# Start, gate rows and last norm of a two-layer encoder trunk: first weight chunk in two DMAs, written order, earlier row loads, TensorE in the last LayerNorm

## The chip, the cores and the metric

The kernel runs on one core of a Trainium2 chip. The metric is the device time of the whole program in microseconds (us), as the median of three runs. A profiled execution has a span (first to last instruction) and a time of its own beside it.

## What is computed

The reference takes 256 frames of width 2048 through two layers. Layer 0 mixes with a gated MLP (gelu, a LayerNorm over 6144 gate channels, a 128x128 masked product over positions, a product with the other half, an output projection); layer 1 with a low-rank attention. After each mixer comes a gated MLP with a causal convolution of width 3. Each sub-layer ends in a LayerNorm. All in float32:

```python
z = gelu(x @ w_in); u, v = split(z, 2)
v = layer_norm(v, ln_g, ln_b)
s = einsum('gij,bnjgd->bnigd', w_s * mask, v) + b_s
m = (u * s) @ w_out                       # layer 0; layer 1: latent attention
x = layer_norm(ALPHA * x + m, ln_mix_g[i], ln_mix_b[i])
f = (silu(conv(x @ w_up)[g]) * conv(x @ w_up)[a]) @ w_down
x = layer_norm(ALPHA * x + f, ln_ffn_g[i], ln_ffn_b[i])   # the last one writes the output
```

## The kernel before, in words

**Products.** Every float32 weight is split on the core into a rounded part (`wh`, a cast on ACT, L131) and a remainder (`wl`, a subtraction on DVE, L134); activations are split in the same way (`xhl` holds both parts side by side). A product is then three TensorE matmuls: hi by hi, lo by hi, hi by lo (`prod_b`, called by `Banks.to`). Some chunks are "seven" chunks, which trade one of eight products for sums of weights made on DVE (`ts`, L141) and split too (`th`, `tl`). 128 rows by 512 columns is one PSUM bank, and eight banks exist.

**Weights.** All weights pass through one list of chunks of 1 MB (`Feed`). SyncE (SP) loads chunk i into one of three `raw` buffers (`_load`, L88 on), ACT and DVE split it (`_split`), TensorE uses it. A load may start when the buffer is free, that is when chunk i-3 has been split, and not before the matmul that was written last ahead of it (`behind`). DVE, ACT and SP each work strictly in the order of their queue; a scheduler makes the order, and some instructions are pinned in the written one.

**Start.** A bf16 tile of zeros is set by GpSimd (POOL), and nine matmuls on it run while nothing has been loaded (L286 on). Then, for the first quarter of x (j = 0), SP is given in this order: x of k = 0; pieces 1 and 2 of chunk 0 (512 columns each); x of k = 1; pieces 3 and 4; x of k = 2 and of k = 3; then chunk 1 in two halves. The interleaving is done by two callbacks, `feed.between` (L324), which `_load` and `_split` call after their second piece. Chunk 0 holds the weights of k = 0 (columns 0 to 1023) and k = 1 (1024 to 2047), chunk 1 those of k = 2 and 3. The 24 matmuls of a chunk are `acc.eight`, in an order that the scheduler chose. POOL also loads the first quarter of the position weights (`wT`, from `in_w_sT_dram`) at that time, through its own software queue.

**The gate v and its rows.** Six groups g of 1024 columns of v are made first (chunks 0 to 47), then six groups of u (chunks 48 to 95). `stats(gi)` (L707) sums the squares of v of one group on ACT; its output tiles are not read, and lie in the pool `t2` of five buffers, which also holds the temporaries of a group's end (`rest`, L442). After the sums of the last group come mean and reciprocal deviation (`mv`, `vrs`). `row_v` (L783) has POOL load one row of 512 of the gate LayerNorm's scale or shift, spread over all partitions, into a `t2` tile `vr`; `norm_v` (L796 and L797) normalises v with them on DVE, in two passes: (v - mean) by scale row, then by `vrs` and plus shift row. For g = 0, these stand before the products of u; for the later groups among them. `spatial(0)` is the position product of group 0 (matmuls on `wT`), behind the third chunk of u (chunk 50). At the end of group 0 of u, `rest` reads four banks on DVE (L448 to L451), and the next group's matmuls write into these banks.

**The end.** The last down projection is finished one row block b (128 frames) and one quarter f (512 columns) at a time. `piece` (L661, L664) adds a quarter to the residual and takes its moments; after the last quarter, `start` aggregates them (L669), ACT takes the square root and DVE the reciprocal; `scale` (L678, L679) is, per quarter, (r - mean) by the scale row `lng` and then by the reciprocal deviation and plus the shift row `lnb`, and SP stores the quarter.

## Time and profile before

| | |
|---|---|
| median of 3 runs | 2469.26 us (2468.65, 2469.26, 2470.97) |
| profiled execution: its own time | 2471.25 us |
| profiled execution: span | 2469.5 us |
| mean granted TensorE clock | 0.998 |
| TensorE (PE) busy | 2453.7 us, 99% of the span, 12481 instructions |
| VectorE (DVE) busy | 2054.2 us, 83% |
| ScalarE (ACT) busy | 1459.5 us, 59% |
| moved from and to HBM | 544.75 MB read, 65.06 MB written |

In a timeline row the first number is the start in us from the span's start, the second the time from the first start to the last end of the instructions in the row, then engine, line, operation, output and inputs, and the count; in brackets stands how long the engine had been idle before it, and what released it. A wait row names the waiting engine and line, what it waited for, the total, the number of waits and the longest. PE is the matmul part of TensorE, PEld its weight loads.

### The profile page before, as it was taken

The numbers are of one execution on the slowest core, as the hardware profiler recorded it, in microseconds if no ns is written. First come the engines' busy times: TensorE is split into PE (matmuls) and PEld (weight loads), VectorE is DVE, ScalarE is ACT, GpSimd is POOL, SyncE is SP. The second block draws the span as 40 slices with busy tenths as digits, with TensorE's granted clock in tenths as the row PEclk, the third lists the DMA queues.
The fourth block names the chain that finished last, engine by engine and source line by source line (L and its number), as shares of the span: only waits on it lengthen the run. The fifth ranks groups of instructions, "written<-read, shape, count | busy, mean of one in ns | idle before, by whom it ended". The sixth has DMA issues, their size and how long they took to land. (4 is left out here: it accounts for less than half of the span.)

```text
span 2469.5 us, 32459 instructions
## 1 busy us (share of the span) xinstructions
PE 2453.7 (99%) x12481; PEld 2091.0 (85%) x12481; DVE 2054.2 (83%) x2734; ACT 1459.5 (59%) x1969; POOL 104.2 (4%) x202
## 2 busy tenths in 40 slices
PE   9999999999999999999999999999999999999998
PEld 7888788888888888888888888988888888888886
DVE  7999899889898788788777897867598787878798
ACT  6666565566565666556655566665565665655453
POOL 0000000000000000000000000000000000000000
PEclk9999999999999999999999999999999999999999
DMA  7555766656665678777868885544478787877885
GB/s 276 204 205 208 231 204 194 217 181 213 206 219 190 230 291 322 297 279 288 330 215 320 303 300 184 193 158 161 172 270 310 273 312 294 300 264 274 300 324 201
DMA packets 117004, 611.94 MB, mean 248 GB/s; under 512 B 10712, under 2 KB 11488, under 8 KB 75760
## 3 DMA queue, kind: packets, MB, share of 16 engines
q1 hardware_dynamic: 90704, 462.47, 52.7%
q0 software_dynamic: 26144, 147.39, 15.9%
q8 instruction: 98, 1.61, 0.3%
q14 instruction: 58, 0.48, 0.1%
HBM read 544.75 MB, written 65.06 MB: 247 GB/s over the span
## 5 line engine op out<-in xcount | busy, mean ns | idle before, releaser
L134 DVE TENSOR_TENSOR wl<-raw,wh 128x1024 fp32r<-128x1024 f32 (+4 forms) x645 | 957.3, 1499 | 176.8 <-ACT wh L131 131.8
L131 ACT CAST wh<-raw 128x1024 fp32r<-128x1024 f32 (+4 forms) x645 | 809.3, 1278 | 362.6 <-PE up L236 85.7
L236 PE MATMUL up<-xhl,wh 128*128 128x512 f32 x2624 | 611.4, 390 | 0.0
L236 PEld LDWEIGHTS up<-xhl,wh 128*128 128x128 f32 x2624 | 487.5, 188 | 97.7
L236 PEld LDWEIGHTS up<-xhl,wl 128*128 128x128 f32 x2624 | 325.8, 192 | 6.4
L236 PE MATMUL up<-xhl,wl 128*128 128x256 f32 x2624 | 328.1, 283 | 0.0
L131 ACT CAST th<-ts 128x1536 fp32r<-128x1536 f32 (+1 forms) x138 | 142.8, 1052 | 113.8 <-DVE ts L141 89.4
L236 PE MATMUL ub<-wh,xhl 128*128 128x512 f32 x576 | 179.5, 393 | 1.9 <-DVE u0w L449 1.9
L134 DVE TENSOR_TENSOR tl<-ts,th 128x1536 fp32r<-128x1536 f32 (+1 forms) x138 | 162.9, 1217 | 10.5 <-ACT th L131 3.6
L236 PEld LDWEIGHTS ub<-wh,xhl 128*128 128x128 f32 x576 | 108.1, 188 | 26.4 <-DVE u0w L449 2.4
L236 PE MATMUL ub<-wl,xhl 128*128 128x512 f32 x288 | 112.2, 389 | 0.0
L141 DVE TENSOR_TENSOR ts<-ts,raw 128x512 f32<-128x512 f32 x138 | 94.5, 684 | 1.4
L141 DVE TENSOR_TENSOR ts<-raw 128x1024 f32<-128x1024 f32 x69 | 84.0, 1218 | 7.7 <-PE ub L236 3.8
L236 PE MATMUL mo<-wh,oT 128*128 128x512 f32 x256 | 82.5, 401 | 0.0
L236 PE MATMUL v_q<-wh,xhl 128*128 128x512 f32 x224 | 70.1, 394 | 1.7 <-ACT wh L131 1.7
L236 PEld LDWEIGHTS ub<-wl,xhl 128*128 128x128 f32 x288 | 54.1, 188 | 11.4
L236 PE MATMUL v_p<-wh,xhl 128*128 128x512 f32 x192 | 60.2, 392 | 0.1
L236 PEld LDWEIGHTS v_q<-wh,xhl 128*128 128x128 f32 x224 | 42.2, 190 | 11.3 <-ACT wh L131 2.7
L236 PEld LDWEIGHTS mo<-wh,oT 128*128 128x128 f32 x256 | 45.5, 189 | 7.1
L236 PE MATMUL mo<-wl,oT 128*128 128x512 f32 x128 | 50.1, 392 | 0.0
L693 ACT ACTIVATE lny<-lnt,lncol 128x128 f32<-128x128 f32 x96 | 36.5, 469 | 15.7 <-PE lnt L689 15.6
L396 DVE TENSOR_TENSOR h_0a<-up,lo_0a 128x256 f32<-128x256 f32 x41 | 17.2, 419 | 32.7 <-ACT lo_0a L394 32.7
(1826 smaller groups left out, 4328.4 us busy)
## 6 DMA issues: line engine op xcount, KB each, us to landing
raw<-in_ffn_up_dram SPq DMA_DIRECT2D x172, 1024.0 KB, 7.1
raw<-in_gm_in_dram SPq DMA_DIRECT2D x93, 1024.0 KB, 5.3
raw<-in_ffn_dn_dram SPq DMA_DIRECT2D x68, 1024.0 KB, 6.9
raw<-in_gm_wout_dram SPq DMA_DIRECT2D x48, 1024.0 KB, 5.2
praw<-in_ffn_dn_dram POOLq DMA_DIRECT2D x16, 1024.0 KB, 15.2
keptth<-pth POOLq DMA_DIRECT2D x16, 1024.0 KB, 8.1
kepttl<-ptl POOLq DMA_DIRECT2D x16, 1024.0 KB, 9.0
fth<-keptth POOLq DMA_DIRECT2D x16, 1024.0 KB, 10.0
```

The lines of the kernel that those rows point to most:

```text
L131: cast = self.nc.scalar.copy(hi, raw)
L134: self.nc.vector.tensor_tensor(lo, raw, hi.bitcast(F32), ALU.subtract)
L141: add = lambda o, a, b: self.nc.vector.tensor_tensor(o, a, b, ALU.add)
L236: recent[0] = nc.tensor.matmul(o, l, r, start=start, stop=stop, skip_group_check=True)
L396: nc.vector.tensor_tensor(h, acc[:, 0:S], lo, ALU.add)
L693: nc.scalar.activation(y[:, j], t[:, j * P : (j + 1) * P], AF.Identity, bias=lncol[:, o : o + 1], scale=lncol[:, g : g + 1])
```

## The change

There are three places.

**Start.** Chunk 0 is loaded in two DMAs of 1024 columns instead of four of 512 and still split in four pieces; x of k = 0 and 1 comes in one DMA ahead of it, x of k = 2 and 3 in one behind it; the callbacks are gone. There are ten matmuls on zeros instead of nine. The matmuls of chunks 0 and 1 (the "first two pairs") are pinned in a written order, `Banks.first`: for each half of the chunk and each 512 columns in it, hi by hi for both row blocks, lo by hi for both, hi by lo for both.

SP's queue at the start of the program, before (`xraw` is x as loaded, `raw` a weight chunk):

```order
L315 DMA xraw_90<-in_xT_dram 128x256
L102 DMA raw_92<-in_gm_in_dram 128x512 x2
L315 DMA xraw_90<-in_xT_dram 128x256
L102 DMA raw_92<-in_gm_in_dram 128x512 x2
L315 DMA xraw_90<-in_xT_dram 128x256 x2
L102 DMA raw_118<-in_gm_in_dram 128x1024 x2
L315 DMA xraw_121<-in_xT_dram 128x512 x2
```

and in the changed kernel:

```order
L310 DMA xraw_91<-in_xT_dram 128x512
L100 DMA raw_93<-in_gm_in_dram 128x1024 x2
L310 DMA xraw_91<-in_xT_dram 128x512
L100 DMA raw_111<-in_gm_in_dram 128x1024 x2
L310 DMA xraw_114<-in_xT_dram 128x512 x2
```

The bytes and their order are the same but for x of k = 1, which has moved ahead of chunk 0; ten DMAs up to the end of chunk 1 have become six.

**Gate rows.** `row_v` for group 0 is called ahead of `stats(5)`, and `stats(5)` writes its unread squares into four PSUM banks of the coming u products (`ub[4:]`) instead of into `t2` tiles. So the rows take the buffers that the temporaries of v's last group leave, not those that the squares leave.

DVE's queue behind the last group of v, before (`v_462` is group 0 of v, `v_774` group 1, `vmv` the means, `vrs` the reciprocal deviations, `vr` the rows, `raw_1950` chunk 51, `raw_2055` chunk 52):

```order
L359 RECIPROCAL vrs_2015<-vrs0q 128x1
L796 SCALAR_TENSOR_TENSOR v_462<-v_462,vmv_2005,vr_2027 128x512
L796 SCALAR_TENSOR_TENSOR v_462<-v_462,vmv_2006,vr_2027 128x512
L797 SCALAR_TENSOR_TENSOR v_462<-v_462,vrs_2015,vr_2029 128x512
L359 RECIPROCAL vrs_2025<-vrs1q 128x1
L796 SCALAR_TENSOR_TENSOR v_462<-v_462,vmv_2005,vr_2031 128x512
L797 SCALAR_TENSOR_TENSOR v_462<-v_462,vrs_2025,vr_2029 128x512
L797 SCALAR_TENSOR_TENSOR v_462<-v_462,vrs_2015,vr_2033 128x512
L796 SCALAR_TENSOR_TENSOR v_462<-v_462,vmv_2006,vr_2031 128x512
L134 TENSOR_TENSOR wl_2082<-raw_1950,wh_2081 128x2048
L797 SCALAR_TENSOR_TENSOR v_462<-v_462,vrs_2025,vr_2033 128x512
L141 TENSOR_TENSOR ts_2115<-raw_2055 128x1024
```

and in the changed kernel (`v_455` is group 0, `v_767` group 1, `raw_1943` chunk 51); two first passes over `v_455` stand just ahead of this piece:

```order
L831 SCALAR_TENSOR_TENSOR v_767<-v_767,vmv_2010,vr_2100 128x512
L821 TENSOR_SCALAR vmv_2011<-vmv_2011 128x2
L822 TENSOR_TENSOR vmv_2011<-vmv_2011,vc 128x1
L831 SCALAR_TENSOR_TENSOR v_455<-v_455,vmv_2011,vr_1998 128x512
L823 TENSOR_TENSOR vmv_2011<-vmv_2011 128x1
L831 SCALAR_TENSOR_TENSOR v_455<-v_455,vmv_2011,vr_2002 128x512
L824 TENSOR_TENSOR vmv_2011<-vmv_2011 128x1
L128 TENSOR_TENSOR wl_2071<-raw_1943,wh_2070 128x2048
L351 RECIPROCAL vrs_2020<-vrs0q 128x1
L831 SCALAR_TENSOR_TENSOR v_767<-v_767,vmv_2011,vr_2100 128x512
L351 RECIPROCAL vrs_2030<-vrs1q 128x1
L832 SCALAR_TENSOR_TENSOR v_455<-v_455,vrs_2020,vr_2000 128x512
```

The first passes have moved ahead of the reciprocals, the split of chunk 51 ahead of the second passes, and a pass over group 1 that needs the fifth row (`vr_2100`) ahead of all of these. ACT's cast of chunk 51 likewise stands ahead of the square roots now.

**Last norm.** For the last row block, `finish` replaces `scale`. With mean m, reciprocal deviation s, scale row g and shift row b, three of the four quarters are computed as r g s + (b - m s g): `weigh` multiplies r by g ahead of the last quarter's piece; TensorE puts b into three PSUM banks by a float32 product with the identity, and adds -m s g by a float32 product with a diagonal matrix `dg`; one pass on DVE per quarter then joins the two. The fourth quarter takes the two passes of before.

DVE's queue from the last two pieces on, before:

```order
L661 TENSOR_TENSOR res_1_20724<-res_1_20724,dn_e 128x512
L664 BN_STATS lnst_1_19367<-res_1_20724 128x6
L661 TENSOR_TENSOR res_1_20724<-res_1_20724,dn_q_20199 128x512
L664 BN_STATS lnst_1_19367<-res_1_20724 128x6
L669 BN_AGGR lnmv_1_21011<-lnst_1_19367 128x2
L678 SCALAR_TENSOR_TENSOR res_0_19894<-res_0_19894,lnmv_1_21011,lng_20772 128x512
L359 RECIPROCAL lnrs_1_21015<-lnrs_1q 128x1
L678 SCALAR_TENSOR_TENSOR res_0_19894<-res_0_19894,lnmv_1_21011,lng_20772 128x512
L679 SCALAR_TENSOR_TENSOR res_0_19894<-res_0_19894,lnrs_1_21015,lnb_20774 128x512 x2
L678 SCALAR_TENSOR_TENSOR res_1_20724<-res_1_20724,lnmv_1_21011,lng_20772 128x512 x2
L679 SCALAR_TENSOR_TENSOR res_1_20724<-res_1_20724,lnrs_1_21015,lnb_20774 128x512 x2
```

and in the changed kernel:

```order
L688 TENSOR_TENSOR res_1_20713<-res_1_20713,lng_20761 128x512
L664 TENSOR_TENSOR res_1_20713<-res_1_20713,dn_q_20188 128x512
L667 BN_STATS lnst_1_19356<-res_1_20713 128x6
L672 BN_AGGR lnmv_1_21009<-lnst_1_19356 128x2
L351 RECIPROCAL lnrs_1_21013<-lnrs_1q 128x1
L699 SCALAR_TENSOR_TENSOR off<-lnmv_1_21009,lnrs_1_21013 128x1
L701 TENSOR_SCALAR dg<-ident,off 128x128
L705 SCALAR_TENSOR_TENSOR res_1_20713<-res_1_20713,lnmv_1_21009,lng_20761 128x512
L706 SCALAR_TENSOR_TENSOR res_1_20713<-res_1_20713,lnrs_1_21013,lnb_20763 128x512
L710 SCALAR_TENSOR_TENSOR res_0_19883<-res_0_19883,lnrs_1_21013,fin_21003 128x512
L710 SCALAR_TENSOR_TENSOR res_0_19883<-res_0_19883,lnrs_1_21013,fin_21004 128x512
L710 SCALAR_TENSOR_TENSOR res_1_20713<-res_1_20713,lnrs_1_21013,fin_21005 128x512
```

Eight passes over 512 columns behind the aggregation have become five, with two small operations ahead of them; three multiplications have moved ahead of the last piece. TensorE has six float32 products more at its end.

The diff, cut to its core:

```diff
@@ Feed._load
-        step = 512 if self.loaded == 0 else cols
...
-            if self.loaded in (1, 2):
-                step = 1024
+            step = 1024 if self.loaded < 3 else cols
             for o in range(0, cols, step):
                 self.behind(self.nc.sync.dma_start(t[:, o : o + step], ap[:, o : o + step]))
-                if self.loaded == 0 and o == step:
-                    self.between[0]()
@@ Feed._split
-            if i == 0 and o == step:
-                self.between[1]()
@@ trunk
-    for _ in range(9):
+    for _ in range(10):
         mm(warm, idle[:, 0:P], idle, True, True)
...
-            feed.between = [lambda: load(slice(1, 2)), lambda: split(slice(1, 2))]
-            load(slice(0, 1))
+            load(slice(0, 2))
             feed.ahead(1, 0)
-            load(slice(2, 3))
-            load(slice(3, 4))
-            split(slice(0, 1))
+            load(slice(2, 4))
+            split(slice(0, 2))
             feed.ahead(1, 1)
-            split(slice(2, 3))
-            split(slice(3, 4))
+            split(slice(2, 4))
@@ Banks
+        def first(self, a, hi, lo, begin):
+            for j in range(2):
+                for f in range(2):
+                    o = slice(j * 1024 + f * 512, j * 1024 + f * 512 + 512)
+                    for n in range(3):
+                        for b in range(2):
+                            tc.keep_in_program_order(mm(self.acc[DIRECT[2 * b + f]], a[b][j][n == 1],
+                                                        (lo if n == 2 else hi)[:, o], begin and j == n == 0, False))
+            self.begun.update(DIRECT)
...
+            elif gi == 0 and c < 2:
+                acc.first(a, *got, c == 0)
             else:
                 acc.eight(a, *got)
@@ Norm
+        def weigh(self, b, f):
+            r = self.r(b, f)
+            tc.keep_in_program_order(nc.vector.tensor_tensor(r, r, self.g[:, f * 512 : (f + 1) * 512], ALU.mult))
+        def finish(self, b):
+            t = [bank(f"fin{f}") for f in range(3)]
+            c = [slice(f * 512, (f + 1) * 512) for f in range(4)]
+            for f in range(3):
+                mm(t[f], ident, self.b[:, c[f]], True, False)
+            self.start(b)
+            pin = tc.keep_in_program_order
+            off = st.tile([P, 1], F32, tag="rstd", name="off")
+            pin(nc.vector.scalar_tensor_tensor(off, self.mu, -1.0, self.rs, ALU.mult, ALU.mult))
+            dg = tp.tile([P, P], F32, tag="t1", name="dg", bufs=T1)
+            pin(nc.vector.tensor_scalar(dg, ident, off, None, op0=ALU.mult))
+            for f in range(3):
+                mm(t[f], dg, self.g[:, c[f]], False, True)
+            r = self.r(b, 3)
+            pin(nc.vector.scalar_tensor_tensor(r, r, self.mu, self.g[:, c[3]], ALU.subtract, ALU.mult))
+            pin(nc.vector.scalar_tensor_tensor(r, r, self.rs, self.b[:, c[3]], ALU.mult, ALU.add))
+            nc.sync.dma_start(out[b * P : (b + 1) * P, c[3]], r)
+            for f in range(3):
+                r = self.r(b, f)
+                nc.vector.scalar_tensor_tensor(r, r, self.rs, t[f], ALU.mult, ALU.add)
+                nc.sync.dma_start(out[b * P : (b + 1) * P, c[f]], r)
@@ gate rows
-    def stats(gi):
+    def stats(gi, junk=None):
-                sq = tp.tile([P, 512], F32, tag="t2", name=f"vsq{gi}{b}{f}", bufs=T2)
+                sq = junk[2 * b + f] if junk else tp.tile([P, 512], F32, tag="t2", name=f"vsq{gi}{b}{f}", bufs=T2)
...
-    stats(5)
+    ub = [bank(f"ub{i}") for i in range(8)]
+    rows0 = [row_v(0, 0), row_v(0, 1)]
+    stats(5, ub[4:])
...
-    for f, rows in enumerate([row_v(0, 0), row_v(0, 1)]):
+    for f, rows in enumerate(rows0):
         norm_v(0, f, rows)
@@ end
     for b in range(2):
-        for f in (2, 3):
-            end(b, f)
-            ln.piece(b, f, acc[b][f])
+        end(b, 2)
+        ln.piece(b, 2, acc[b][2])
+        if b == 1:
+            for f in range(3):
+                ln.weigh(b, f)
+        end(b, 3)
+        ln.piece(b, 3, acc[b][3])
+        if b == 1:
+            ln.finish(b)
+            break
         ln.start(b)
```

More of the change, by code (lines that the diff above doesn't have):

```diff
@@ L236, in mm @@
         recent[0] = nc.tensor.matmul(o, l, r, start=start, stop=stop, skip_group_check=True)
+        return recent[0]
     def order(later, earlier):
@@ L769, in trunk, with row_v @@
             nc.scalar.copy(bsc, bst[:, 0:NG])
-    stats(5)
+    def row_v(g, f):
+        got = []
+        for i in range(2):
+            t = tp.tile([P, 512], F32, tag="t2", name=f"vr{g}{f}{i}", bufs=T2)
+            nc.gpsimd.dma_start(t, gbd[12 * i + 2 * g + f : 12 * i + 2 * g + f + 1, :].to_broadcast([P, 512]))
+            got.append(t)
+        return got
+    ub = [bank(f"ub{i}") for i in range(8)]
+    rows0 = [row_v(0, 0), row_v(0, 1)]
+    stats(5, ub[4:])
     mv = [st.tile([P, 4], F32, tag="vmv", name=f"vmv{b}", bufs=2) for b in range(2)]
@@ L781, in trunk @@
         vrs.append(rstd_of(mv[b][:, 1:2], 0, f"vrs{b}"))
-    def row_v(g, f):
-        got = []
-        for i in range(2):
-            t = tp.tile([P, 512], F32, tag="t2", name=f"vr{g}{f}{i}", bufs=T2)
-            nc.gpsimd.dma_start(t, gbd[12 * i + 2 * g + f : 12 * i + 2 * g + f + 1, :].to_broadcast([P, 512]))
-            got.append(t)
-        return got
     def norm_v(g, f, rows):
@@ L803, in trunk @@
     acts = Acts(pT, "wo", NF_GM)
-    ub = [bank(f"ub{i}") for i in range(8)]
     def spatial(g, tiles):
```

## The prediction

> **What bounds the kernel now.** I read the page's busy times first, then TensorE's waits, then the timelines at the three places that the change touches.

> ```profile
> PE 2453.7 (99%) x12481; PEld 2091.0 (85%) x12481; DVE 2054.2 (83%) x2734; ACT 1459.5 (59%) x1969; POOL 104.2 (4%) x202
> ```
> ```profile
> PE ub L236 <- DVE u0w L449: 1.9, 1, 1.9
> ```

> TensorE is busy for 99% of the span. So DVE, ACT or DMA time is worth something only where it makes TensorE stand, or run slowly, and behind its last matmul. The sum of all that is small. A matmul in an unhindered stretch comes every 5.44 / 24 = 0.2267 us, by this piece of the chain that ended last:

> ```profile
> 2448.15 5.44 PE dn_e L236 x24
> ```

> At the start, TensorE's timeline shows nine matmuls on zeros, six real ones, a gap, and eight at half speed:

> ```profile
> 1.32 4.02 PE L236 MATMUL warm<-idle 128*128 128x512 bf16 x9 [1.32 <-POOL idle L286]
> 4.99 0.99 PE L236 MATMUL v_q<-wh,xhl 128*128 128x512 f32 x2
> ...
> 6.89 0.40 PE L236 MATMUL v_e<-wh,xhl 128*128 128x512 f32 x1
> 9.00 1.22 PE L236 MATMUL v_q<-wh,xhl 128*128 128x512 f32 x2 [1.72 <-ACT wh L131]
> ...
> 12.51 0.40 PE L236 MATMUL v_e<-wl,xhl 128*128 128x512 f32 x1
> ```

> The granted clock (the number behind the engines' busy times, then DMA share and GB/s) says why the eight are slow:

> ```profile
> 4.00:6.00 2.00, 1.98 (x6) 0.66 (x4) 0.82 (x2) 1.21 (x2) 0.00 (x0) 1.00 1.07 220
> ...
> 10.00:12.00 2.00, 2.00 (x6) 1.59 (x5) 1.02 (x3) 1.16 (x2) 0.00 (x0) 0.50 1.04 414
> ```

> Fourteen real matmuls stand ahead of 12.51, and from there none is late for a long time. At full pace they are worth 14 x 0.2267 = 3.17 us, so the start costs 12.51 - 3.17 = 9.34 us. The half clock is 1.70 of it: eight matmuls from 9.00 to 12.51 take 3.51 instead of 1.81.

> **Start, step by step.** ACT's casts show when each DMA had landed:

> ```profile
> 3.26 0.41 ACT L319 CAST xhl<-xraw 128x256 fp32r<-128x256 f32 x1 [1.25 <-DMA xraw<-in_xT_dram]
> 4.32 0.62 ACT L131 CAST wh<-raw 128x512 fp32r<-128x512 f32 x1 [0.65 <-DMA raw<-in_gm_in_dram]
> 5.41 0.62 ACT L131 CAST wh<-raw 128x512 fp32r<-128x512 f32 x1 [0.47 <-DMA raw<-in_gm_in_dram]
> 7.68 0.41 ACT L319 CAST xhl<-xraw 128x256 fp32r<-128x256 f32 x1 [1.65 <-DMA xraw<-in_xT_dram]
> 8.33 1.29 ACT L131 CAST wh<-raw 128x512 fp32r<-128x512 f32 x2 [0.24 <-DMA raw<-in_gm_in_dram]
> ...
> 11.07 1.05 ACT L131 CAST wh<-raw 128x1024 fp32r<-128x1024 f32 x1 [0.84 <-DMA raw<-in_gm_in_dram]
> 12.35 1.06 ACT L131 CAST wh<-raw 128x1024 fp32r<-128x1024 f32 x1 [0.22 <-DMA raw<-in_gm_in_dram]
> ```
> ```profile
> 12.15 1.23 DVE L134 TENSOR_TENSOR wl<-raw,wh 128x1024 fp32r<-128x1024 f32 x1 [1.14 <-ACT wh L131]
> ```

> In KB landed up to each row that is 128, 384, 640, 768, 1024, 2048 and 2560. The bytes of the changed queue come in nearly the same order, so I place its DMAs by their last byte. x of k = 0 and 1 ends at 256 KB, between 3.26 and 4.32, and is cast long before it is needed. The first half of chunk 0 ends at 768 KB. From above that is 7.68, where x of k = 1 landed. From below it is 5.41 plus half of the 1.09 us that the 256 KB before took, 5.95. I take 5.95: the half is the second and third DMA slot of before, and the row nearest to it is piece 2, which came through on time, while the slow stretch (220 GB/s) held what was queued behind it. [...] The second half ends at 1280 KB, a quarter of the way from 8.33 to 11.07, 9.0.

> A matmul starts 0.67 behind a landing (4.32 to 4.99). So the first twelve, all on the first half, start at 6.65 and end at 9.35. The next twelve start at 9.0 + 0.67 = 9.7 and end at 12.4. Chunk 1 has its first cast at 11.07 + 1.05 = 12.1 and its remainder at 13.35, and four matmuls (0.9) need the cast alone, so nothing waits again. 24 x 0.2267 = 5.44 back from 12.4 is 6.98: the start is worth 9.34 - 6.98 = 2.36 us. Ten matmuls on zeros end 0.43 later, at 5.77, so the idle stretches are 0.9 and 0.35, against the 1.72 that lost the clock. Best: the second half in time too, 9.34 - 6.65 = 2.7. Worst: 7.68 + 0.67 = 8.35 behind 2.6 idle, with the same 1.70 of half clock, 10.05, a loss of 0.7. [...] The written order of the matmuls alone costs and gains nothing: it has as many.

> **Gate rows.** The only long wait of TensorE is that at 306.97. Engines in order of the chain:

> ```profile
> 292.94 0.61 PE L236 MATMUL ub<-wh,xc 128*128 128x512 f32 x2
> ...
> 304.64 0.39 PE L236 MATMUL ub<-wl,xhl 128*128 128x512 f32 x1
> 306.97 0.73 PE L236 MATMUL ub<-wh,xhl 128*128 128x512 f32 x2 [1.94 <-DVE u0w L449]
> ```
> ```profile
> 258.36 0.68 DVE L755 TENSOR_TENSOR v<-v_q,v5u 128x512 f32<-128x512 f32 x1
> ...
> 269.73 0.75 DVE L796 SCALAR_TENSOR_TENSOR v<-v,vmv,vr 128x512 f32<-128x512 f32 x1 [3.03 <-DMA vr<-gbrows]
> ...
> 272.38 2.28 DVE L134 TENSOR_TENSOR wl<-raw,wh 128x2048 fp32r<-128x2048 f32 x1
> ...
> 294.92 0.68 DVE L134 TENSOR_TENSOR tl<-ts,th 128x512 fp32r<-128x512 f32 x1
> ...
> 305.08 1.22 DVE L141 TENSOR_TENSOR ts<-raw 128x1024 f32<-128x1024 f32 x1 [2.15 <-DMA raw<-in_gm_in_dram]
> 306.23 0.68 DVE L449 TENSOR_TENSOR u0w<-ub,u0u 128x512 f32<-128x512 f32 x1
> ```
> ```profile
> 298.00 0.37 SPq L97 DMA_DIRECT2D raw<-in_gm_in_dram  x1
> ```
> ```profile
> 261.55 0.54 POOL L788 DMA_DIRECT2D vr<-gbrows  x1 [0.91 <-ACT vsq L713]
> ```

> Read backwards: L449 stands in DVE's queue behind the first sum of chunk 58, whose load was issued at 298.00 and landed 7.05 us later. The issue waited for the split of chunk 55, which DVE began when it was through with chunk 54 at 295.6. DVE was late there because it had stood 3.03 us for a gate row, issued at 261.55.

> In the changed kernel the rows take buffers that DVE leaves by 258.36 + 0.68 = 259.04, so the third goes out near 259.1 and the fifth near 260.5, instead of 261.55 and 262.96 (one more issue every 0.7). The 3.03 should go. By the new order DVE then does five first passes and the split of chunk 51 before the second passes; at 0.67 a pass, with the fifth row at 265.2, it ends that split at 269.7 (before: 274.66), the last second pass of group 0 at 273.1 (the position products start at 273.81), and chunk 54 near 292 (before 295.6). Chunk 55's split needs a buffer that TensorE leaves at 292.94, so it ends at 295.2; the load of chunk 58 goes out 2.75 earlier, lands at 302.3 instead of 305.05, and L449 ends at 306.91 - 2.75 = 304.15. TensorE asks for its bank at 304.64 + 0.23 = 304.87. The wait goes whole, 306.97 - 304.87 = 2.1 us, with a margin of 0.7. What is late next is nothing near: DVE is earlier by more than TensorE. Bounds: 2.1 if all holds; 0 if the load's landing does not move with its issue; below nothing, see the last rival. Writing squares to PSUM instead of SBUF has no row; it has the same passes on ACT, and 11 us before the banks are used, which is cover enough. The fp32 position products themselves do not change.

> **Last norm.**

> ```profile
> 273.81 3.60 PE L236 MATMUL ub<-v,wT 128*128 128x512 f32 x12
> 277.06 0.81 PE L236 MATMUL ub<-wh,xhl 128*128 128x512 f32 x2
> ...
> 2458.64 0.39 PE L236 MATMUL dn_q<-wl,dn11wx 128*128 128x512 f32 x1
> ```
> ```profile
> 13.30 0.28 DVE L297 TENSOR_TENSOR xs<-xraw 128x128 f32<-128x128 f32 x1
> ...
> 2459.07 0.69 DVE L661 TENSOR_TENSOR res<-res,dn_q 128x512 f32<-128x512 f32 x1 [2.35 <-PE dn_q L236]
> ...
> 2460.51 0.26 DVE L669 BATCH_NORM_AGGREGATE lnmv<-lnst 128x2 f32<-128x24 f32 x1
> ...
> 2461.48 0.16 DVE L359 RECIPROCAL lnrs<-lnrs_1q 128x1 f32<-128x1 f32 x1
> ...
> 2463.53 1.41 DVE L678 SCALAR_TENSOR_TENSOR res<-res,lnmv,lng 128x512 f32<-128x512 f32 x2
> 2464.85 1.41 DVE L679 SCALAR_TENSOR_TENSOR res<-res,lnrs,lnb 128x512 f32<-128x512 f32 x2
> ```
> ```profile
> 2460.81 0.29 ACT L357 ACTIVATE lnrs_1q<-lnmv,epsc 128x1 f32<-128x1 f32 x1 [10.58 <-DVE lnmv L669]
> ```

> Before, eight passes follow the aggregation (over at 2460.77), 0.66 apart (2463.53 to 2464.85 for two), and end at 2466.26. Now the square root ends at 2461.1; reciprocal and `off` take 0.2 each, `dg` at most the 0.28 of a 128x128 operation: 2461.8. Five passes of 0.66 end at 2465.2, 1.05 sooner. The last store, 3.2 us from there to the end, moves with it. The three multiplications by the scale row (at most 0.7 each, 2.1) fit the 2.35 in which DVE stands ahead of 2459.07. TensorE has the four 512 columns' worth of position products from 273.81 to 277.06, 0.81 per float32 product of 512: three by the identity run to 2461.3, three on `dg` end at 2462.7, 2463.5 and 2464.4, and the pass that needs the last of them starts at 2461.8 + 4 x 0.66 = 2464.45. Just covered. At half clock they would take 1.62 each, and the end would come 1.2 later than before: the bounds are +1.05 and -1.2. I take 1.05, since TensorE stands 0.6 only.

> **The sum.** Against the profiled execution's own time: 2471.25 - 2.36 - 2.1 - 1.05 = 2465.7. The median of the runs is 2469.26, 1.99 below that execution, and the runs lie at 2468.65, 2469.26 and 2470.97: a step of about the 1.70 that the half clock costs. If the two fast ones kept the clock, the start is worth 0.66 there instead of 2.36. I take the middle, 1.5: 2469.26 - 1.5 - 2.1 - 1.05 = **2464.6** for the median. A measurement can tell about 0.2%, 4.9 us, from no change; that bound lies at 2464.3.

> **Rivals.** (1) *The start is worth all of 2.36 to 2.7 in the median too*: 2469.26 - 5.5 to 5.85, 2463.4 to 2463.8. For it: the half clock may belong to every run. Against: the spread of the runs. 0.18. (2) *The load decides at 304.87.* The rows come early, but chunk 58's load still lands near 305, since chunks 59 and 60 are loaded beside it or chunk 55 waits longer for its buffers; the change then does not do what it says there. 7.05 us for 1 MB says that the load is slowed by something. 2466.7. 0.2. (3) *Chunk 0 lands at 7.68* and the clock is lost as before: a start that is worth -0.7 against the profiled execution and -2.4 against a run that kept its clock, middle -1.5: 2467.6. For it: the landing at 768 KB in the trace is that one. 0.12. (4) *DVE's queue is blocked by the fifth gate row*, which ends slower than before. That pass stands now ahead of everything that the position products need. They bear a landing up to 267.4; each us beyond it stops TensorE for one, and the wait at 306.97 then stays. A row took 261.55 to 269.73, 8.2 us; that would be 268.7 here, a stop of 1.3. It outweighs the 2.55 gained at the start and end from 270 on; at 272.0 it costs 4.6: 2469.26 - 2.55 + 4.6 = 2471.3. Against: four of the five rows are out before the next 1 MB load is asked for. 0.04.

> The forecast has 0.46, by itself 2463.7 to 2465.6. The range takes in rivals 1 to 3: 2462.9 to 2467.9. Faster by over 0.2%: rival 1 and a third of the forecast, 0.33. Slower by over 0.2% needs 2474.2, beyond rival 4's price: 0.02. Within: 0.65.

> **What would show it.** Right: first real matmul near 6.65, full clock throughout, no wait of DVE on `vr`, no wait of TensorE on L449, a DVE that ends about 6.2 us behind TensorE's last down product instead of 7.2. Wrong: a first cast of chunk 0 behind 7.5; a granted clock of 0.50 before 14 us; `spatial` matmuls waiting for L832; last passes waiting for TensorE's `fin` products.

## The result and the profile after

The changed kernel takes 2465.82 us (median of 20 runs, 2464.91 to 2466.43), the kernel before 2470.74 us in 20 runs beside them (2468.65 to 2472.71): ratio 0.9982, 95% interval 0.9976 to 0.9988, 4.92 us less. The runs of before spread over 4.1 us, those of the changed kernel over 1.5. The profiled execution has a span of 2464.6 us and a time of its own of 2466.37, 4.88 below before's.

In the changed kernel TensorE's waits, behind the 1.3 us ahead of its first matmul, are these; of the two of before (1.9 on L449 and 1.7 at the start) the first is gone and the second down to 0.3, and a new one of 0.3 stands in the last norm:

```profile
PE fin L230 <- DVE dg L701: 0.3, 1, 0.3
PE v_q L230 <- ACT wh L125: 0.3, 1, 0.3
```

The start, ACT's casts first (each shows a landing), then TensorE:

```profile
4.16 0.62 ACT L314 CAST xhl<-xraw 128x512 fp32r<-128x512 f32 x1 [2.14 <-DMA xraw<-in_xT_dram]
5.36 1.14 ACT L125 CAST wh<-raw 128x512 fp32r<-128x512 f32 x2 [0.58 <-DMA raw<-in_gm_in_dram]
8.32 1.14 ACT L125 CAST wh<-raw 128x512 fp32r<-128x512 f32 x2 [1.82 <-DMA raw<-in_gm_in_dram]
...
10.82 1.05 ACT L125 CAST wh<-raw 128x1024 fp32r<-128x1024 f32 x1 [0.84 <-DMA raw<-in_gm_in_dram]
```
```profile
1.31 4.45 PE L230 MATMUL warm<-idle 128*128 128x512 bf16 x10 [1.31 <-POOL idle L281]
6.03 0.50 PE L230 MATMUL v_q<-wh,xhl 128*128 128x512 f32 x1 [0.27 <-ACT wh L125]
...
8.99 0.50 PE L230 MATMUL v_q<-wh,xhl 128*128 128x512 f32 x1
...
11.62 0.39 PE L230 MATMUL v_q<-wl,xhl 128*128 128x512 f32 x1
11.92 0.50 PE L230 MATMUL v_q<-wh,xhl 128*128 128x512 f32 x1
...
13.18 0.50 PE L230 MATMUL v_q<-wl,xhl 128*128 128x512 f32 x1
```

The first half of chunk 0 is there at 5.36, the second at 8.32. The 24 matmuls on chunk 0 start from 6.03 to 11.62, 0.4 us more than the full pace (23 x 0.2267 = 5.21); chunk 1 adds two small pauses, at 11.92 and 13.18. The granted clock, the number behind the engines' busy times, is 1.00 in the stretch in which it was 0.50 before:

```profile
10.00:12.00 2.00, 2.00 (x10) 1.39 (x8) 0.96 (x3) 1.05 (x1) 0.00 (x0) 1.00 1.04 411
```

The gate rows and what hangs on them: POOL's issues, DVE, SP's load of chunk 58, and TensorE at the bank that DVE's L452 (L449 before) empties:

```profile
255.03 2.18 POOL L808 DMA_DIRECT2D vr<-gbrows  x4 [0.67 <-DVE v L788]
```
```profile
260.86 0.75 DVE L831 SCALAR_TENSOR_TENSOR v<-v,vmv,vr 128x512 f32<-128x512 f32 x1 [1.76 <-DMA vr<-gbrows]
...
262.19 0.75 DVE L831 SCALAR_TENSOR_TENSOR v<-v,vmv,vr 128x512 f32<-128x512 f32 x1 [0.51 <-DMA vr<-gbrows]
...
263.84 0.75 DVE L831 SCALAR_TENSOR_TENSOR v<-v,vmv,vr 128x512 f32<-128x512 f32 x1 [0.76 <-DMA vr<-gbrows]
...
291.23 4.73 DVE L128 TENSOR_TENSOR wl<-raw,wh 128x2048 fp32r<-128x2048 f32 x2
...
299.96 1.23 DVE L135 TENSOR_TENSOR ts<-raw 128x1024 f32<-128x1024 f32 x1 [0.88 <-DMA raw<-in_gm_in_dram]
301.10 0.68 DVE L452 TENSOR_TENSOR u0w<-ub,u0u 128x512 f32<-128x512 f32 x1
```
```profile
293.55 0.37 SPq L96 DMA_DIRECT2D raw<-in_gm_in_dram  x1
```
```profile
271.42 3.60 PE L230 MATMUL ub<-v,wT 128*128 128x512 f32 x12
...
302.11 0.62 PE L230 MATMUL ub<-wh,xhl 128*128 128x512 f32 x2
...
306.19 3.59 PE L230 MATMUL ub<-v,wT 128*128 128x512 f32 x8
```

DVE still stands 3.03 us in all for gate rows (1.76 + 0.51 + 0.76), but from 259 on and not from 266.7 on. The bank is free at 301.78 and asked for at 302.11: no wait.

The end:

```profile
2454.70 0.69 DVE L664 TENSOR_TENSOR res<-res,dn_q 128x512 f32<-128x512 f32 x1 [0.57 <-PE dn_q L230]
...
2457.17 0.28 DVE L701 TENSOR_SCALAR dg<-ident,off 128x128 f32<-128x128 f32 x1
2457.38 0.74 DVE L705 SCALAR_TENSOR_TENSOR res<-res,lnmv,lng 128x512 f32<-128x512 f32 x1
2458.16 0.75 DVE L706 SCALAR_TENSOR_TENSOR res<-res,lnrs,lnb 128x512 f32<-128x512 f32 x1
2458.82 2.32 DVE L710 SCALAR_TENSOR_TENSOR res<-res,lnrs,fin 128x512 f32<-128x512 f32 x3
```
```profile
2454.27 0.40 PE L230 MATMUL dn_q<-wl,dn11wx 128*128 128x512 f32 x1
2454.51 2.74 PE L230 MATMUL fin<-lnb,ident 128*128 128x512 f32 x6
2457.51 2.84 PE L230 MATMUL fin<-lng,dg 128*128 128x512 f32 x6 [0.27 <-DVE dg L701]
```

I cut each profiled execution at four events: TensorE's first position product of group 0 (271.42 here, 273.81 before), that of group 1 (306.19 here; 311.18 before), its last down product (2454.27; 2458.64) and the end of DVE's last pass (2461.14; 2466.26). The stretches are:

| kernel (profiled execution) | start to group 0 | to group 1 | to the last down product | to DVE's last pass | to the end |
|---|---|---|---|---|---|
| before | 273.81 | 37.37 | 2147.45 | 7.62 | 3.22 |
| changed | 271.42 | 34.77 | 2148.07 | 6.87 | 3.45 |
| start alone | 271.98 | 36.59 | 2147.60 | 7.62 | 3.46 |
| gate rows alone | 271.14 | 34.77 | 2148.18 | 7.62 | 3.23 |
| last norm alone | 273.95 | 36.77 | 2147.49 | 6.87 | 3.23 |
| before, sixteen on zeros | 273.32 | 36.87 | 2147.78 | 7.62 | 3.21 |
| before, POOL's load held | 271.43 | 38.69 | 2147.53 | 7.63 | 3.22 |
| changed, POOL's load held | 271.63 | 34.77 | 2147.65 | 6.88 | 3.45 |
| changed, rows asked for late in the code | 271.19 | 34.79 | 2147.56 | 6.88 | 3.46 |
| changed, two quarters on TensorE | 270.90 | 34.77 | 2147.52 | 7.28 | 3.52 |
| changed, one DMA less | 270.68 | 34.77 | 2148.08 | 6.87 | 3.02 |
| changed, both | 270.95 | 34.77 | 2147.44 | 6.87 | 3.01 |
| changed, no written order | 271.22 | 34.77 | 2147.99 | 6.87 | 3.44 |
| changed, five on zeros | 271.93 | 34.77 | 2147.45 | 6.87 | 3.46 |

So from before to the changed kernel the profiled executions differ by -2.39 (start), -2.60 (gate rows), +0.62 (something late, new), -0.75 (last passes) and +0.23 (behind the last pass): -4.9 in all.

### The profile page after: what moved, and what is told of

Same layout as the page of the kernel before. It is cut to its first block, busy times and chain, and to the rows that moved or that the text cites. A ratio compares the mean times of both kernels' runs of the same rounds, so it can differ in the third digit from the quotient of the medians.

```text
span 2464.6 us, 32483 instructions
## 1 busy us (share of the span) xinstructions
PE 2458.1 (100%) x12494; PEld 2091.3 (85%) x12494; DVE 2054.7 (83%) x2734; ACT 1459.3 (59%) x1967; POOL 104.2 (4%) x202
```

## The experiments

Each group of four ran on one chip, beside 30 to 33 runs of the kernel before.

**The start alone.** The hunks of the start, nothing else:

```diff
+            step = 1024 if self.loaded < 3 else cols
-    for _ in range(9):
+    for _ in range(10):
+            elif gi == 0 and c < 2:
+                acc.first(a, *got, c == 0)
```

> The kernel before with the start alone changed (order of the first loads, ten matmuls on zeros, first two pairs in the written order). Theory, the parts add: the position products of group 0, which began at 273.81 before and at 271.42 after, begin 2.4 us sooner, the wait on L449 stays near 2 us, and the time falls by 2.4 us. Rival 1, the load of chunk 58 lands when it did, whatever TensorE does: the wait on L449 grows to about 4.3 us and the time falls by 0.4 or less. Rival 2, my step from the profiled execution to the median (some executions of the kernel before keep the full clock): 1.5 us in the median.

2468.04 us (11 runs) against 2469.54 (33 runs), 1.50 less; ratio 0.9994, interval 0.9985 to 1.0002. The position products begin at 271.98, 1.8 sooner than before. TensorE's wait for the load of chunk 58 moved with TensorE and did not grow:

```profile
304.35 0.72 PE L230 MATMUL ub<-wh,xhl 128*128 128x512 f32 x2 [1.51 <-DVE u0w L452]
```

Rival 1 falls: 36.59 us between the two position products, as in the kernels with the old start. The median agrees with rival 2, my 1.5, but its interval does not tell 1.5 from the theory's 2.4.

**The gate rows alone.**

```diff
+    ub = [bank(f"ub{i}") for i in range(8)]
+    rows0 = [row_v(0, 0), row_v(0, 1)]
-    stats(5)
+    stats(5, ub[4:])
```

> The kernel before with the gate rows alone changed (squares into PSUM banks, rows asked for ahead of the statistics). Theory: the wait of TensorE on L449 and the small pauses near 295 go, 2.6 us less. The prediction had 2.1. Rival, the load of chunk 58 decides and its landing does not move with its issue: under 0.5 us less.

2468.05 us, 1.49 less in the median; ratio 0.9993, interval 0.9984 to 1.0002. The wait is gone, and 34.77 us stand between the position products, against 36.59 to 37.37 in four kernels without this part. The 11 runs fall into two groups, 2466.56 to 2467.10 (five) and 2468.05 to 2469.60 (six). The profiled execution, of the lower group, has the old start, and yet keeps its clock and comes to the position products at 271.14, sooner than the changed kernel. Its third and fourth pieces of chunk 0 were cast at 7.22 (8.33 before), so that TensorE had no pause over 0.44 us there:

```profile
6.25 0.51 PE L236 MATMUL v_p<-wh,xhl 128*128 128x512 f32 x1 [0.34 <-ACT wh L131]
...
7.89 0.73 PE L236 MATMUL v_q<-wh,xhl 128*128 128x512 f32 x2 [0.44 <-ACT wh L131]
```

**The last norm alone.**

```diff
+            if b == 1:
+                ln.finish(b)
+                break
```

> The kernel before with the last norm alone changed. The prediction: 1.05 us less behind TensorE's last down product. What the profile after shows: from that product's start to the end 10.33 us instead of 10.86, so 0.5 us less. Of the small waits of TensorE in the last 30 us of the down product, which cost 0.57 us in the profile after: if they come with this part, they show here too and the time stays within 0.2 us of before; if they are chance or come from running earlier, they don't.

2468.34 us, 1.20 less in the median; ratio 0.9998, interval 0.9989 to 1.0006. In the profile, 6.87 us from the last down product to DVE's last pass instead of 7.62: 0.75. No small waits in the down product. The start of this execution lost its clock, as that of the kernel before did:

```profile
5.10 0.86 PE L236 MATMUL v_q<-wh,xhl 128*128 128x512 f32 x2
7.92 0.50 PE L236 MATMUL v_p<-wh,xhl 128*128 128x512 f32 x1 [1.96 <-ACT wh L131]
```

The three medians add to 4.19 us of the 4.92; the interval of each alone is some 2 us to either side and takes in no change, so the medians do not tell whether they add, and I go by the stretches.

**Sixteen matmuls on zeros in the kernel before.**

```diff
-    for _ in range(9):
+    for _ in range(16):
```

> The kernel before with sixteen matmuls on zeros instead of nine, and nothing else. They end near 8.4, so TensorE has no pause of 1.7 us. Theory, the pause costs the clock: no half clock in any stretch, the first real matmul near 8.45 and the start worth 9.34 - 8.45 = 0.9 us, and a spread of the runs as small as after's (1.5 us instead of 4.1). Rival, the clock falls there for another reason (the real matmuls, or so many us from the program's start): the half clock stays, and with the real matmuls 3.5 us later the time is 0.5 to 2 us more.

2469.99 us, 0.45 more in the median (ratio 1.0003, interval 0.9994 to 1.0011), the runs from 2469.51 to 2471.39. The zeros end at 7.37, the clock stays, and still TensorE waits for the third piece of chunk 0, which ACT casts behind x of k = 1 (7.99):

```profile
7.02 0.82 PE L236 MATMUL v_q<-wh,xhl 128*128 128x512 f32 x2
...
9.33 0.74 PE L236 MATMUL v_q<-wh,xhl 128*128 128x512 f32 x2 [1.25 <-ACT wh L131]
```

The theory holds on the clock (no half clock behind its first rise) and on the spread of the runs, 1.9 us against 4.5 for the kernel before on the same chip. On the gain it holds by half: real matmuls that could have run at 5 come behind zeros, and the position products begin at 273.32. That is 0.5 better than before, where I expected 0.9, and 2.2 worse than the execution at 271.14, which kept its clock and had its pieces sooner. The median does not tell a gain of this size.

**POOL's first load held back in the kernel before.** A copy of one column of v makes it wait for group 0:

```diff
                     t = tp.tile([P, 2, P], F32, tag="t1", name=f"wT{i}", bufs=T1)
+                    if i == 0: nc.gpsimd.tensor_copy(t[:, 0, 0:1], v[0][:, 0, 0:1])
                     nc.gpsimd.dma_start(t, w_sT[:, 2 * i : 2 * i + 2, :])
```

> The kernel before, with the first load of position weights on POOL's queue held back until the v result of group 0 is there (near 55 us); nothing else. Theory: that load is what delays x of k = 1 and the pieces behind it; they land near 6.2 and 7 instead of 7.7 and 8.3, TensorE has no pause over 1 us, keeps its clock, and its position products begin near 271 instead of 273.8. The runs then no longer fall into two groups 1.9 us apart (on the chip of the first four experiments 19 of 33 at 2468.0 to 2469.6, 14 at 2470.2 to 2472.5), and the median falls by 1.5 us or more, as much as by the whole change of the start. Rival, the two groups come from where the clock's windows happen to lie against the pause: the landings stay and so do the groups, 0.3 us or less.

2468.81 us, 0.53 less in the median; ratio 0.9998, interval 0.9990 to 1.0007. x of k = 1 is cast at 5.95 (6.55, 7.68, 7.99 and 8.10 in the four old starts without the hold), and the position products begin at 271.43. But two groups remain (eight runs to 2469.60, three from 2470.27), and the profiled execution, of the upper group, shows why: it lost the clock in the other pause, at L449. TensorE there, and a window with the granted clock (0.50, the number behind the engines' busy times):

```profile
304.29 0.99 PE L236 MATMUL ub<-wh,xhl 128*128 128x512 f32 x2 [1.95 <-DVE u0w L449]
305.07 0.63 PE L236 MATMUL ub<-wl,xhl 128*128 128x512 f32 x1
```
```profile
306.00:308.00 2.00, 2.00 (x6) 1.58 (x5) 2.00 (x5) 1.94 (x4) 0.00 (x0) 0.50 0.49 172
```

38.69 us between the position products, 1.8 more than the mean of the four with the same wait and a kept clock (36.90). Theory and rival are both half right: the load does delay x of k = 1, and in the profiled executions the clock was lost at two places.

The executions without the hold fit this. The traces list the packets of every DMA and, for each of these loads, sixteen counts of a semaphore. In the kernel before, four packets of POOL's load (4 KB each) took 2.5 us, and four of the sixteen counts of x of k = 1 came at 7.58 to 7.66, the other twelve by 6.61; its cast began at 7.68. With sixteen matmuls on zeros one such packet took 2.9 us, and one count came at 7.97, the others by 6.62. With the last norm alone three took 1.9 to 3.0 us, and the counts straggle up to 8.07. With the gate rows alone no packet took over 1.7 us, and all counts were there by 6.53.

**The same hold in the changed kernel** (the same line).

> The changed kernel with the same hold on POOL's first load. Theory: the second half of chunk 0 (8.32 in the profile after) lands near 7, TensorE runs from 6.0 without a pause, its position products begin near 270.8 instead of 271.4, and the time is 0.6 us below the changed kernel's. Rival, the transfers are as slow there for another reason (the queue has just started): the second half still lands past 8 and nothing changes. The small waits in the last down product (0.55 us from the first to the last of the two groups, seen in both kernels with the gate rows asked for early and in none of four without): if they belong to that part, 2148.1 us from the position products of group 1 to the last down product; if they were chance, 2147.6.

2465.35 us; against before 0.9983 (0.9975 to 0.9992). The second half of chunk 0 is cast at 8.79, no sooner. Over the new starts it came between 6.65 and 9.37 with no hold, and at 6.76 and 8.79 with it. A few late counts set it: in each of these nine executions eight of its sixteen counts are there by 6.22, and the last comes anywhere from 6.63 to 9.35; here thirteen are there by 6.40, and the other three come at 7.28, 8.54 and 8.76, with no packet of POOL beside them. Why a count is late there stays open. The rival stands for this execution. The small waits at the end are absent (2147.65).

**Rows asked for late in the code.**

```diff
-    rows0 = [row_v(0, 0), row_v(0, 1)]
     stats(5, ub[4:])
...
+    rows0 = [row_v(0, 0), row_v(0, 1)]
     for f, rows in enumerate(rows0):
```

> The changed kernel with the two calls that ask for the first gate rows back behind the statistics in the code; the squares still go to PSUM banks. Theory, the buffers alone decide when a row is asked for: rows on POOL's queue between 253.8 and 257.2 as in the profile after, 34.8 us from the position products of group 0 to those of group 1, and the changed kernel's time. Rival, the place in the code decides (the rows take the queue and DVE's order with them): the first rows come 4 us or more later, TensorE waits on L452 again, up to 2 us more.

2465.67 us, 0.9984 (0.9975 to 0.9993). POOL issues as in the changed kernel, and the position products lie 34.79 apart:

```profile
253.80 0.54 POOL L808 DMA_DIRECT2D vr<-gbrows  x1 [195.90 <-ACT wh L125]
255.00 2.19 POOL L808 DMA_DIRECT2D vr<-gbrows  x4 [0.67 <-DVE v L788]
```

The buffers decide, not the place in the code: writing the squares to PSUM gives all of this part by itself. The other half, early calls with the squares still in `t2`, was not run.

**Two quarters on TensorE instead of three.**

```diff
-            for f in range(3):
+            for f in range(2):
                 mm(t[f], dg, self.g[:, c[f]], False, True)
...
+            for f in (3, 2):
+                r = self.r(b, f)
```

> The changed kernel with two quarters of the last norm on TensorE instead of three; DVE does the fourth and the third in two passes each. Theory, in the changed kernel the last three passes wait for the float32 products (0.785 apart in the profile after, where TensorE's products are 0.86 apart) and not for PSUM: here they follow a long done TensorE and come 0.66 apart, six passes end 7.4 us behind the last down product (6.87 with three quarters, 7.62 without). Rival, a pass that reads PSUM takes 0.79 by itself: 7.5 to 7.6. Time, 0.5 to 0.7 us more than the changed kernel.

2465.82 us, 0.9985 (0.9977 to 0.9994). TensorE is through at 2458.41, and the passes on PSUM (L711) come 0.66 behind one another like all others:

```profile
2457.75 0.75 DVE L706 SCALAR_TENSOR_TENSOR res<-res,lnmv,lng 128x512 f32<-128x512 f32 x1
2458.41 0.74 DVE L711 SCALAR_TENSOR_TENSOR res<-res,lnrs,fin 128x512 f32<-128x512 f32 x1
2459.07 0.75 DVE L707 SCALAR_TENSOR_TENSOR res<-res,lnrs,lnb 128x512 f32<-128x512 f32 x1
```

7.28 us to DVE's last pass, between 7.62 and 6.87; the medians do not tell this 0.4 us. So in the changed kernel it is TensorE that spaces the last three passes 0.785 apart on the mean; the chain that ended last goes through TensorE there:

```profile
2457.51 2.86 PE fin L230 x6
...
2460.39 0.75 DVE res L710
```

**One DMA less on the sync queue.**

```diff
-            load(slice(0, 2))
-            load(slice(2, 4))
+            if j == 3:
+                load(slice(0, 4))
+            else:
+                load(slice(0, 2))
+                load(slice(2, 4))
```

> The changed kernel with the last 1 MB of the activations' first half-row loads, the two of the fourth tile, asked for in one DMA instead of two: one DMA less on the sync queue, and nothing else moves. Theory: at the end the sync engine checks its eight DMA counters in a fixed order, 0.06 us each; the counter of the last store is the second of ten checks in the changed kernel (eight follow) and the seventh in the kernel before, which is why the end lies 3.45 us behind the last pass of DVE in five kernels with the new start and 3.22 in five without. One DMA less makes it the last counter: 3.0 us, 0.4 us less in all. Rival, the 0.23 belongs to something else of the new start: 3.45 stays.

The edit joins the two DMAs of 256 KB of the last quarter of x (512 KB in all) into one. 2465.36 us against 2470.09 (30 runs); ratio 0.9980, interval 0.9971 to 0.9989. The end lies 3.02 us behind the last pass, not 3.45. The sync engine's checks at the end in the trace (start in us from DVE's last pass; S100 to S110 are counters of its own DMAs, in brackets the one of the last store):

```
before:       S118 0.46  S100 0.52  S101 0.58  S103 0.64  S104 1.52  [S106] 2.15  S107 2.21  S109 2.27  S110 2.33
changed:      S118 0.40  [S100] 2.14  S102 2.20  S103 2.26  S105 2.32  S107 2.38  S108 2.44  S109 2.50  S110 2.57
one DMA less: S118 0.41  S100 0.47  S102 0.53  S103 0.60  S105 0.66  S107 0.72  S108 0.78  S109 1.31  [S110] 2.14
```

The check on the last store is passed at 2.14 or 2.15 in all three. What follows it in the list is paid for, 0.06 each: seven checks in the changed kernel (I had counted eight), three before, none with one DMA less. The theory stands.

**Both, a try at a faster version** (one DMA less, and POOL's load held).

> The changed kernel with that DMA less and with POOL's first load of position weights held back as well: a try at a faster version. Theory: the end as in the kernel with one DMA less, 0.4 us; the hold was worth 0 to 0.3 us in the median of the changed kernel, so 0.4 to 0.7 us below the changed kernel (near 2465.2 beside a kernel before of 2469.5 to 2470.7). Rival: no more than the one DMA brings.

2464.76 us (nine runs, 2464.06 to 2465.57); ratio 0.9976, interval 0.9966 to 0.9985. Its median is the lowest of all, 0.60 below that with one DMA less on the same chip, whose runs (2464.58 to 2465.60) overlap with these. In this execution the second half landed at 6.76. Whether the hold does more than shift the odds of that landing stays open.

**No written order for the first two pairs.**

```diff
-            elif gi == 0 and c < 2:
-                acc.first(a, *got, c == 0)
```

> The changed kernel with the scheduler's order of the matmuls for the first two pairs again. The prediction: the written order costs and gains nothing, since the matmuls are as many; the position products of group 0 begin between 270.9 and 272.0 as in five kernels with it. Rival, the order matters since it uses the cast parts of a half as soon as they are there: TensorE waits for casts between 6 and 12 us, and the products begin 0.5 to 1 us later.

2466.61 us, 0.9983 (0.9975 to 0.9992), runs from 2465.56 to 2467.88. The kernel with one DMA less ran beside it, and without its 0.43 at the end it would be at 2465.79: the order seems worth 0.8 in the median, and the runs spread wider without it. The profiled execution does not show it (271.22, within the range with the order), since its second half came as soon as 6.65. The median speaks for the rival, but its mechanism was not seen.

**Five matmuls on zeros.**

```diff
-    for _ in range(10):
+    for _ in range(5):
```

> The changed kernel with five matmuls on zeros instead of ten, which end near 3.5. Theory, the full clock is granted at the end of a window of 3.41 us in which TensorE worked nearly all the time, and the windows lie at another place in every execution: with a pause of 2.3 us there is none before the real matmuls, the first window of full clock begins between 9.4 and 12.8, and ten or more real matmuls run at half clock, 0.2 us more each: 2 to 3.5 us more, by another amount in each run. Rival, the first transfers bound the start anyway: under 0.5 us more.

2467.05 us, 0.9987 (0.9978 to 0.9996), 1.3 above the 2465.79. Eight real matmuls run at half clock, 0.43 apart, until 9.33:

```profile
5.57 0.79 PE L230 MATMUL v_q<-wh,xhl 128*128 128x512 f32 x1 [1.95 <-ACT wh L125]
...
8.73 0.63 PE L230 MATMUL v_q<-wh,xhl 128*128 128x512 f32 x1
9.15 0.47 PE L230 MATMUL v_p<-wh,xhl 128*128 128x512 f32 x1
```

The mechanism is the theory's, at 1.3 instead of 2 to 3.5 us in the median. In this execution, one of the fastest of the eleven (2466.29, 0.5 above the 2465.79), the second half of chunk 0 came at 8.76, and the twelve matmuls of the first half would have waited for it anyway. A slower one was not profiled. What the tenth matmul on zeros and the joined DMAs are each worth was not run by itself.

## Why the prediction was right, point by point

**Start: the size held, in part by luck, and the account of it was too simple.** I had 2.36 against the profiled execution; it was 2.39 (273.81 to 271.42). The two landings came sooner than placed by bytes (5.36 for 5.95, 8.32 for 9.0), and the pauses on chunk 0 and those at 11.92 and 13.18, which I had ruled out, gave most of it back. Another execution would have given another number: with the new start and ten matmuls on zeros the position products begin anywhere from 270.68 to 271.98. I took 1.5 for the median, since some executions of before keep the clock; the start alone measured 1.50, give or take 2. The old start came to the position products at 271.14 when it kept its clock and at 273.81 and 273.95 when it lost it. Of these 2.7 us the half clock is 1.7; the rest goes with pieces that came 1.1 later (8.33 against 7.22). Of the four executions with nine matmuls on zeros three lost the clock behind its first rise, one of them at L449; of the eight with the new start and ten none did.

The 5.95, chosen over 7.68, was my estimate from the rows of before. In the old start, x of k = 1, which is asked for at 2.12, behind POOL's load at 1.82, was held up by it: in the one execution with that load held it was cast 0.6 to 2.2 us sooner than in the four without, and there the late counts go with the load's slow packets. The second half of chunk 0 in the new start is asked for ahead of it, at 1.64, and its casts at 8.79 and 6.76 with the load held lie within the range without.

**"The written order alone costs and gains nothing"**: not borne out. Taking it away cost some 0.8 us in the median, by a way that one profile did not show.

**Gate rows: the result held, a step in it did not.** I had 2.1; the stretch fell by 1.8 to 2.6 us in the pairs of executions that kept their clock there (mean 36.90 to 34.77, 2.1). "The 3.03 should go" is the step that failed: DVE stands for the rows as long as before, only 5 us sooner against TensorE's work, where it has room. It was through with chunk 54 only 2.0 us sooner against TensorE (291.23 + 2.39 = 293.6, before 295.6), where I had 3.6 (near 292). The load of chunk 58 went out 2.06 sooner (298.00 - 2.39 - 293.55) and not 2.75, and landed after 6.4 us instead of 7.05; the two misses cancel by luck, and the bank was free at 301.78, where I had 304.15 - 2.39 = 301.76. The margin was 0.33, half of my 0.7: the next thing late is this same load. Rival 2 (the landing does not move with its issue) fell.

**Last norm: mis-sized.** 1.05 predicted; 0.75 to DVE's last pass. All up to `dg` fitted (2457.45 against 2461.8 - 4.37 = 2457.43). The term that was too small is the five passes: 3.76 instead of 3.4. The last three wait for TensorE, whose float32 products take 0.86 each and not 0.81; "just covered" was short by 0.12 a pass, and the first two depend on each other and are 0.78 apart.

**The signs.** The first real matmul at 6.03, the full clock and no wait on L449 came as named. But DVE did wait on `vr`, the last passes did wait for the `fin` products, which I had named as a sign of being wrong, and DVE ended 6.5 us behind the end of the last down product, not 6.2.

**Not foreseen.** 0.23 us behind the last pass, from the number of DMAs on the sync queue. And 0.62 us in the last 30 us of the down product, where a weight load landed 0.9 later against TensorE than before (cast at 2425.03, and 2429.04 before, where TensorE was 4.94 behind). DVE has no break from the split of that load on, and the `dn13wx` that it makes comes late:

```profile
2433.98 0.69 DVE L488 TENSOR_TENSOR dn13wx<-act,dn13wx 128x512 fp32r<-128x512 f32 x1
```
```profile
2434.21 0.39 PE L230 MATMUL dn_p<-wl,dn13wx 128*128 128x512 f32 x1
2434.72 0.50 PE L230 MATMUL dn_q<-wh,dn13wx 128*128 128x512 f32 x1
```

Four of nine profiled executions with early gate rows have it (2147.99 to 2148.18), and of five without (2147.45 to 2147.78) only the one with sixteen matmuls on zeros shows the last two of its small pauses, 0.05 us each. It isn't caused by that part alone, since the other five of the nine don't have it. Whether it makes it likelier stays open.

**The level.** The sum against the profiled execution gave 2465.7, and that execution's counterpart is at 2466.37: the 0.3 of the norm, the 0.23 and the 0.62, less the 0.5 that the gate rows gave more than their 2.1 there. The median of before was 2470.74 over 20 runs, not the 2469.26 of the three that I had. So the change in the median, 4.66 as I had it, came out at 4.92, and the median at 2465.82 instead of 2464.6. The 2.39 and 2.60 of the profiled executions are more than the medians of the single parts show (1.50 and 1.49, each give or take 2). For the start that fits an execution of before that lost the clock there; the 2.60 is large because the stretch of before was the longest of the four with a kept clock (37.37; the others 36.59 to 36.87).

## What to carry to other kernels

TensorE is busy for 99% here, and in the execution of before a pause of 1.72 us cost twice, once as a pause and once as 3.41 us at half clock behind it (1.70 us lost), while one of 1.94 us later in it left the clock as it was. So a kernel whose runs spread over two groups is worth reading pause by pause, in more than one execution. A wait for a small load can be set by the buffer that it lands in: here sending results that nobody reads to another memory freed it, and the place of the call in the code did nothing. When a part's gain is read from one profiled execution, cut several executions at the same events and compare stretch by stretch; the intervals of the medians were wider here than the parts.

## What the runs showed of the hardware

```profile
5.58:9.00 3.42, 1.60 (x6) 0.68 (x5) 1.22 (x4) 1.47 (x3) 0.00 (x0) 1.00 0.91 302
9.00:12.41 3.41, 3.41 (x8) 2.73 (x9) 2.27 (x5) 2.35 (x5) 0.00 (x0) 0.50 1.02 403
```
```profile
303.22:306.64 3.42, 1.78 (x8) 1.15 (x8) 2.56 (x4) 2.46 (x2) 0.00 (x0) 1.00 1.02 393
306.64:310.05 3.41, 3.41 (x17) 2.80 (x16) 3.41 (x7) 2.60 (x5) 0.54 (x1) 1.00 0.72 229
```

- **At the end of these programs the sync engine passed its DMA counters one by one**, 0.06 us each (2.14 to 2.57 us for the last eight in the changed kernel), in the same order in the changed kernel and with one DMA less: which counter the last store got was worth 0.43 us there (3.45 to 3.02).
- **The first loads showed sixteen counts each, and one late count delayed the cast.** In the changed kernel, fifteen counts of the second half of chunk 0 are there by 7.78 and the last at 8.29, and ACT's cast begins at 8.32. In the kernel with one DMA less, fifteen counts of the second half of chunk 0 are there by 6.38 and the last at 6.82; with five matmuls on zeros, thirteen by 6.34 and the last at 8.73.
- **A DVE pass that reads one of its float32 inputs from PSUM took no longer than one on SBUF** (two quarters on TensorE): 0.74 to 0.75, and 0.66 from start to start, in both.
